# Residual update of a block moved into the next in-projection, and an out-projection of both halves at once

## The chip, the cores and the metric

The kernel runs on one core of a Trainium2 chip. The metric is the device time of one execution in microseconds (us), as a median over runs. Five engines work side by side: TensorE (PE; PEld is its weight load), VectorE (DVE), ScalarE (ACT), GpSimd (POOL) and SyncE (SP), on whose queue all the transfers stand. They meet through semaphores.

## The reference

Two layers (DEPTH) of a mixer with adaLN conditioning, over 2048 tokens of 1024 channels, in float32. Cut to what matters:

```python
for l in range(DEPTH):
    shift, scale, gate = split(silu(c) @ w_ada[l] + b_ada[l], 3)
    h = rms_norm(x, g_pre[l]) * (1 + scale) + shift
    u_a, b_a, c_a, gate_a, u_p, gate_p = split(h @ w_in[l])
    y_a = b_a * conv3(c_a * u_a, w_conv[l]) * silu(gate_a)
    y_p = pool(u_p, w_pool[l], pool_scale[l]) * silu(gate_p)
    y = concat([y_a, y_p]) @ w_out[l]
    x = x + gate * rms_norm(y, g_post[l])
```

Each of the six parts of the in-projection is 512 wide. The convolution and the pooling (windows of 2, 4, 8 and 16 tokens) look back in time.

## The kernel before

**Layout and stages.** x lies transposed: channels on the 128 partitions (KT = 8 channel tiles), tokens along the free axis. Work goes in four blocks: layer 0 and 1, each with two blocks of TB = 1024 tokens (two halves of HS = 512). A block has an in-projection, `in_phase`, and an out-projection. The in-projection has 24 groups of 128 output columns (six kinds, four of each); a group is one block of weights against the normalised h of both halves. The product is made in three passes (high x high, high x low, low x high), as every float32 operand is split into a part of the matmul's type and the rest: `mm_k` (L257) issues 8 channel tiles x 3 passes x 2 halves = 48 matmuls of 512 columns for a group. Each group is evicted and mixed on ACT and VectorE by the `use_` functions, ending in y, split in its turn.

**Weights.** `load_w` loads 512 KB (raw), ACT casts the high part (L98), and POOL subtracts for the low part (L108), in two halves of the contraction.

**Out-projection.** `out_half` goes over the eight groups of w_out for one half of the tokens, 24 matmuls a group, and is called twice for a block, so that w_out is loaded twice. Its result stays in SBUF in eight yo tiles. The epilogue, put off by `later` and released by `tick` during the groups that follow, makes 1 / rms of y (`rsqrt_mean`: a matmul with ones, Ln and Exp on ACT, one Newton step on VectorE), then for each channel tile y times it (L435), times the gate plus x (L436), the square (ACT L204) and its sum (VectorE L205) for the next layer's norm, and writes x1 to DRAM.

**Prenorm.** Between the two calls, the main loop queues the prenorm of the next block by `later`: x is loaded again, L234 on VectorE scales it, L235 on ACT adds the shift and rounds to h's high part, L240 on VectorE makes the low part.

**Order.** The scheduler sorts each engine's instructions; `pin` keeps a few in program order. The start (`start`, block 0) is in hand-written order on TensorE, VectorE and ACT: it works on half 0 as inputs arrive. Seven groups of weights are resident by its end; `in_phase` then runs half 1 for them. The last block (`out_last`) keeps w_out on chip and does its second half in two quarters of 256 columns. `background` is a list of steps (w_up times w_pool, adaLN rows, x statistics) handed out over the groups of an in-projection.

**Pools.** PSUM has eight banks: six single tiles for products (psm) and two for the rest (psa). `wsp` has four buffers of half a block of weights, `xpool` three buffers of two channel tiles, `t2` fifteen temporaries of 528 columns.

Of the kernel before, what the change touches and what calls it, by code (L numbers as in the profile page):

```python
# [9 lines left out]
I32 = mybir.dt.int32  # L10
# [3 lines left out]
P = 128  # L14
# [16 lines left out]
RSQRT_SEED = 1597463007.0  # L31
# [3 lines left out]
def trunk(ctx: ExitStack, tc: tile.TileContext, xt, c, wada, vec, rcp, win, wupt, wpool, wout, out):  # L35
# [5 lines left out]
    wsp = ctx.enter_context(tc.tile_pool(name="wsp", bufs=4))  # L41
    xpool = ctx.enter_context(tc.tile_pool(name="xpool", bufs=3))
    t2 = ctx.enter_context(tc.tile_pool(name="t2", bufs=15))
    dram = ctx.enter_context(tc.tile_pool(name="dram", bufs=1, space=bass.MemoryType.DRAM))
    psm = ctx.enter_context(tc.tile_pool(name="psm", bufs=6, space=bass.MemoryType.PSUM))
    psa = ctx.enter_context(tc.tile_pool(name="psa", bufs=2, space=bass.MemoryType.PSUM))

    def tmp(name, dtype=F32):
        return t2.tile([P, HALO + HS], dtype, tag="t", name=name)
# [23 lines left out]
    x1 = [dram.tile([P, KT, HS], F32, name=f"x1_{s}") for s in range(T // HS)]  # L73
# [36 lines left out]
    def load_w(src, dst=None, raw=None, defer=None, behind=None):  # L110
# [16 lines left out]
        return ws
# [29 lines left out]
    def rsqrt_short(ps, n, r, between=None):
        """1 / sqrt(ps + eps) by a short chain: exp(-ln / 2) and one Newton step."""
# [10 lines left out]
        newton(r, v, a, 1)  # L169
        return r  # L170

    def mean_begin(acc, e_hi=nc.vector, e_lo=nc.vector):
        ah = tmp("ah", F32R)
        al = tmp("al", F32R)
        split(acc, ah[:, :HS], al[:, :HS], e_hi, e_lo)
        return ah[:, :HS], al[:, :HS]

    def mean_mm(parts):
        ps = psa.tile([P, HS], F32, tag="aux", name="ps_stat")
        pin(nc.tensor.matmul(ps, lhsT=ones, rhs=parts[0], start=True, stop=False))  # L180
        pin(nc.tensor.matmul(ps, lhsT=ones, rhs=parts[1], start=False, stop=True))
        return ps

    def rsqrt_mean(parts, name, short):
        """1 / sqrt(mean + eps) on every partition, from the split sums of squares per partition."""
        ps = mean_mm(parts)
        if short:
            return rsqrt_short(ps, HS, tmp(name)[:, :HS])
        v = tmp("rs_v")[:, :HS]
        nc.vector.tensor_scalar(v, ps, EPS, None, op0=ALU.add)  # L190
        r = tmp(name)[:, :HS]
        a = tmp("rs_a")[:, :HS]
        nc.vector.tensor_scalar(a.bitcast(I32), v.bitcast(I32), 1, None, op0=ALU.logical_shift_right)
        nc.vector.tensor_scalar(r.bitcast(I32), a.bitcast(I32), -1.0, RSQRT_SEED, op0=ALU.mult, op1=ALU.add)
        newton(r, v, a, 3)
        return r

    def accumulate_sq(acc, src, first):
# [20 lines left out]
    def x_stats(s):
        acc = tmp("xacc")[:, :HS]  # L220
# [527 lines left out]
```

## Time and profile before

| | |
|---|---|
| median of 3 runs | 1516.43 us (1515.33 to 1517.26) |
| profiled execution, its span from first to last instruction | 1513.6 us |
| mean granted TensorE clock | 0.987 |
| TensorE busy | 1461.3 us, 97% of the span |
| VectorE busy | 871.0 us, 58% |
| ScalarE busy | 431.6 us, 29% |
| GpSimd busy | 473.7 us, 31% |
| chain that ended last | PE 79%, DVE 16% |
| DMA | 169.49 MB, 112 GB/s on average |

The profiled execution has no time of its own beside its span; the span leaves out what lies before the first and after the last instruction. Busy shares are averages over stages with different limits. The chain that ended last is followed back from the last instruction to what released it. The ends of matmuls are modelled, so that TensorE can look busy where it runs slowly; matmuls counted in a stretch tell more than its busy time. The granted clock is given as a share of 2.4 GHz.

### The profile page before, as it was taken

Reading aid. Unit: us, or ns where it says so; the run is one execution under the profiler, and the core shown is the slowest. Engines: PE = TensorE matmul, PEld = TensorE weight load, DVE = VectorE, ACT = ScalarE, POOL = GpSimd, SP = SyncE. Lnnn points to the kernel's source line nnn. Section 1 sums busy time; section 2 is a strip of 40 time slices with the busy share of each in tenths; the row PEclk is TensorE's granted clock in tenths of the full one; section 3 lists DMA queues with packets and bytes.
Section 4 is the critical chain, followed back from the end, with each engine's and each line's share of the span. In section 5 each row is a group of like instructions: output and inputs, shape, how many; then the busy total and the mean of one; then the engine's idle time right before and its main releaser. Section 6 shows DMA issues by size and latency. Waiting matters only on the chain.

```text
span 1513.6 us, 16929 instructions
## 1 busy us (share of the span) xinstructions
PE 1461.3 (97%) x6532; PEld 1197.0 (79%) x6532; DVE 871.0 (58%) x1253; ACT 431.6 (29%) x743; POOL 473.7 (31%) x324
## 2 busy tenths in 40 slices
PE   8899999999899999999979999999989999999996
PEld 4688888887678888888858888888867888888896
DVE  7962453869994556362799753352289434425155
ACT  4231211254632121114463121112444111111421
POOL 4510322244432222224534222223433222222501
PEclk9999999999999999999999999999999999999998
DMA  7421233443663332232465321111365411111223
GB/s 307 161 84 53 88 113 102 131 136 117 218 213 119 97 98 90 91 112 84 148 223 172 125 70 56 42 56 56 98 202 181 132 42 56 42 56 42 84 71 110
DMA packets 57684, 169.49 MB, mean 112 GB/s; under 512 B 5634, under 2 KB 9730, under 8 KB 57604
## 3 DMA queue, kind: packets, MB, share of 16 engines
q1 hardware_dynamic: 57604, 168.41, 33.8%
q8 instruction: 51, 0.84, 0.2%
q14 instruction: 29, 0.24, 0.0%
HBM read 147.42 MB, written 20.97 MB: 111 GB/s over the span
## 4 chain that ended last, share of the span: by engine, by line
PE 79%; DVE 16%; issue 2%; DMA 1%; ACT 1%; SPq 0%; DVEq 0%; ACTq 0%
PE ps_in L257 63%; PE ps_out L257 14%; DVE xin L234 3%; DVE h L240 2%; DVE xin L436 1%; DVE ada L130 1%; DVE yo L435 1%; DVE yacc L205 1%; DVE x L234 1%; PE ps_wu L286 1%; DVE rs_a L154 1%; DVE xacc L205 1%; DVE rs_a L153 1%; DVE rn L155 1%; DMA xin<-x 0%
## 5 line engine op out<-in xcount | busy, mean ns | idle before, releaser
L257 PE MATMUL ps_in<-h,ws 128*128 128x512 f32 x4368 | 1008.2, 392 | 22.9 <-ACT h L235 17.6
L257 PEld LDWEIGHTS ps_in<-h,ws 128*128 128x128 f32 x4368 | 822.4, 189 | 202.3 <-ACT h L235 22.6
L108 POOL TENSOR_TENSOR ws<-raw,ws 128x512 fp32r<-128x512 f32 x282 | 420.2, 1493 | 949.0 <-ACT ws L98 949.0
L98 ACT CAST ws<-raw 128x512 fp32r<-128x512 f32 x282 | 174.2, 621 | 572.6 <-PE ps_in L257 297.6
L257 PE MATMUL ps_out<-y,ws 128*128 128x512 f32 (+1 forms) x1296 | 291.5, 384 | 10.8 <-ACT ws L98 6.0
L257 PEld LDWEIGHTS ps_out<-y,ws 128*128 128x128 f32 x1296 | 237.7, 189 | 62.9 <-ACT ws L98 8.2
L205 DVE TENSOR_TENSOR yacc<-yacc,sq 128x512 f32<-128x512 f32 (+1 forms) x62 | 57.2, 923 | 111.9 <-ACT sq L204 111.6
L322 DVE COPY hu<-u 128x16 f32<-128x16 f32 x32 | 5.6, 176 | 178.7 <-ACT u L321 177.8
L368 DVE TENSOR_TENSOR cv<-cv,sga 128x512 f32<-128x512 f32 x32 | 21.9, 724 | 125.3 <-ACT sga L367 125.3
L343 DVE SCALAR_TENSOR_TENSOR pd<-pd,vecs,sgp 128x512 f32<-128x512 f32 x32 | 24.1, 795 | 81.0 <-ACT sgp L342 81.0
L257 PE MATMUL ps_out<-y,wh 128*128 128x256 f32 (+1 forms) x432 | 68.0, 319 | 0.0
L257 PEld LDWEIGHTS ps_out<-y,wh 128*128 128x128 f32 x432 | 61.9, 191 | 5.7
L257 PE MATMUL ps_in<-h,w 128*128 128x512 f32 x240 | 60.1, 401 | 1.0 <-DVE z L353 0.9
L234 DVE SCALAR_TENSOR_TENSOR xin<-xin,apre,rn 128x512 f32<-128x512 f32 x48 | 54.2, 1174 | 3.9 <-DMA xin<-x 3.9
L363 DVE TENSOR_TENSOR cv<-ps_in,cv 128x512 f32<-128x512 f32 x32 | 20.8, 685 | 61.6 <-PE ps_in L257 61.6
L257 PEld LDWEIGHTS ps_in<-h,w 128*128 128x128 f32 x240 | 46.7, 195 | 11.9 <-DVE z L353 1.4
L436 DVE SCALAR_TENSOR_TENSOR xin<-yo,gg,xin 128x512 f32<-128x512 f32 x56 | 52.3, 965 | 1.9 <-DMA xin<-x 1.2
L327 DVE TENSOR_TENSOR win<-win 128x525 f32<-128x525 f32 (+2 forms) x48 | 49.3, 1026 | 1.4
L422 ACT COPY yo<-ps_out 128x512 f32<-128x512 f32 x56 | 32.5, 580 | 58.1 <-PE ps_out L257 58.0
L235 ACT ACTIVATE h<-xin,mod 128x512 fp32r<-128x512 f32 x48 | 33.9, 723 | 42.2 <-DVE xin L234 42.2
L435 DVE TENSOR_TENSOR yo<-yo,ry 128x512 f32<-128x512 f32 x56 | 44.7, 833 | 0.2
L130 DVE SCALAR_TENSOR_TENSOR adaw<-adaw,cb 128x1024 f32<-128x1024 f32 x32 | 44.2, 1388 | 0.0
(112 smaller groups left out, 898.7 us busy)
## 6 DMA issues: line engine op xcount, KB each, us to landing
raw<-win SPq DMA_DIRECT2D x80, 512.0 KB, 3.5
raw<-wout SPq DMA_DIRECT2D x56, 512.0 KB, 3.5
adaw<-wada SPq DMA_DIRECT2D x32, 512.0 KB, 4.0
xin<-xt SPq DMA_DIRECT2D x32, 512.0 KB, 4.5
xin<-x SPq DMA_DIRECT2D x28, 512.0 KB, 4.3
ada<-wada SPq DMA_DIRECT2D x16, 512.0 KB, 8.9
raw<-wu SPq DMA_DIRECT2D x16, 512.0 KB, 3.2
x<-xin SPq DMA_DIRECT2D x16, 512.0 KB, 3.4
```

Of the source, the lines that this page charges most:

```text
L98: i = nc.scalar.copy(hi, src)
L108: e_lo.tensor_tensor(lo, src, hi.bitcast(F32), op=ALU.subtract)
L130: return nc.vector.scalar_tensor_tensor(w, w, 1.0, cb, op0=ALU.mult, op1=ALU.mult, accum_out=mod[:, l, j : j + 1])
L205: nc.vector.tensor_tensor(acc, acc, q, op=ALU.add)
L234: nc.vector.scalar_tensor_tensor(u, u, apre[:, l, k : k + 1], r, op0=ALU.mult, op1=ALU.mult)
L235: nc.scalar.activation(hs[k // 2][:, 0, k % 2, :], u, AF.Identity, bias=mod[:, l, k : k + 1])
L240: nc.vector.scalar_tensor_tensor(lo, u, mod[:, l, k : k + 1], hi, op0=ALU.add, op1=ALU.subtract)
L257: nc.tensor.matmul(ps[s], lhsT=ws[k // KH][:, wi, k % KH, :], rhs=rhs(k, ri, s), start=first and (wi, ri) == PASSES[0], stop=last and (wi, ...
L327: nc.vector.tensor_tensor(nxt[:, lo:], cur[:, lo:], cur[:, lo - w : HALO + HS - w], op=ALU.add)
L422: nc.scalar.copy(t, ps)
L435: nc.vector.tensor_tensor(yo[k], yo[k], r, op=ALU.mult)
L436: nc.vector.scalar_tensor_tensor(t[:, kk], yo[k], gg[:, l, k : k + 1], t[:, kk], op0=ALU.mult, op1=ALU.add)
```

## The change

1. `out_half` becomes `out_phase`: one pass over w_out for both halves (48 matmuls a group), with pair tiles in PSUM of two banks each, three for products and one for the rest.
2. In it, gated y (times gg) goes to DRAM (`ysp`) from ACT, group by group, and its squares are summed. The prenorm of the next block is done here too, in groups 1 to 4; the statistics of its x are ready by then: made in the background of the in-projection, by `x_stat_step` for block 1 and by `finish_steps` for layer 1.
3. `finish_steps`: eight steps in the background of the next in-projection load y and x of a channel tile, multiply by 1 / rms, add, write x1 (or the output), square and accumulate. Two buffers serve them in turn.
4. Work on VectorE and ACT is 1024 wide where it was 512. Temporaries: eight of 1040 columns.
5. The low parts of weights are made on VectorE, 1024 wide (in the start still on POOL). `wsp` has two buffers of a whole block.
6. The groups of the in-projection go in the order ua, up, ca, gp, ba, ga for each i, except in the first block. The split of y has its high part on ACT.
7. `rsqrt_mean`'s long form (an integer seed and three Newton steps) goes; Identity on ACT makes mean + eps.
8. `out_last`: its first half is updated 1024 wide behind group 0 of the first quarter; POOL has no part in the update any more.

The core of the diff:

```diff
-    wsp = ctx.enter_context(tc.tile_pool(name="wsp", bufs=4))
+    wsp = ctx.enter_context(tc.tile_pool(name="wsp", bufs=2))
-    t2 = ctx.enter_context(tc.tile_pool(name="t2", bufs=15))
+    t2 = ctx.enter_context(tc.tile_pool(name="t2", bufs=8))
-    psm = ctx.enter_context(tc.tile_pool(name="psm", bufs=6, space=bass.MemoryType.PSUM))
-    psa = ctx.enter_context(tc.tile_pool(name="psa", bufs=2, space=bass.MemoryType.PSUM))
+    psm = ctx.enter_context(tc.tile_pool(name="psm", bufs=3, space=bass.MemoryType.PSUM))
+    psa = ctx.enter_context(tc.tile_pool(name="psa", bufs=1, space=bass.MemoryType.PSUM))
...
+    IN_ORDER = [(kind, i) for i in range(NCG) for kind in ("ua", "up", "ca", "gp", "ba", "ga")]
...
+    def out_phase(l, b, y, nl, nb):
+        acc = tmp("yacc")[:, :TB]
+        log_exp()
+        h = []
+        rn = None
+        for j in range(KT):
+            ws = load_w(wout[l, j])
+            ps = pair_ps("ps_out")
+            for n, k in enumerate(range(KT) if j else OUT_ORDER):
+                mm_k(ws, [ps[:, 0], ps[:, 1]], y_rhs(y, 0, HS), k, n == 0, n == KT - 1)
+            if j == 0:
+                st = mean_mm(xparts[nl, nb])
+                rn = rsqrt_short(st, TB, tmp("rn")[:, :TB])
+            pf = flat(ps)
+            t = tmp("yg")[:, :TB]
+            nc.scalar.activation(t, pf, AF.Copy, scale=gg[:, l, j : j + 1])
+            accumulate_sq(acc, pf, j == 0)
+            nc.sync.dma_start(ysp[l, b][:, j], t)
+            for k in ((), (0, 1), (2, 3), (4, 5), (6, 7), (), (), ())[j]:
+                hk = hpool.tile([P, 2, TB], F32R, tag=f"h{k}", name=f"h{k}")
+                h.append(hk)
+                u = xpool.tile([P, TB], F32, tag="x", name="xin")
+                nc.sync.dma_start(u, x_src(nl, k, nb * TB, TB))
+                prenorm_hi(hk[:, 0], nl, k, u, rn)
+                prenorm_lo(hk[:, 0], hk[:, 1], nl, k, u)
+        parts = mean_begin(acc)
+        return parts, lambda k, ri, s: h[k][:, ri, s * HS : (s + 1) * HS]
...
+    def finish_steps(l, b):
+        st = {}
+        def step(k):
+            e = ypool.tile([P, 2, TB], F32, tag=("y3", "y7")[k % 2], name="fin")
+            nc.sync.dma_start(e[:, 0], ysp[l, b][:, k])
+            nc.sync.dma_start(e[:, 1], x_src(l, k, b * TB, TB))
+            nc.vector.tensor_tensor(e[:, 0], e[:, 0], ry[l, b], op=ALU.mult)
+            nc.vector.tensor_tensor(e[:, 1], e[:, 1], e[:, 0], op=ALU.add)
+            if l + 1 < DEPTH:
+                nc.sync.dma_start(x1[b][:, k], e[:, 1])
+                if k == 0:
+                    st["acc"] = tmp("xacc")[:, :TB]
+                accumulate_sq(st["acc"], e[:, 1], k == 0, e[:, 0])
+                if k == KT - 1:
+                    xparts[l + 1, b] = mean_begin(st["acc"])
+            else:
+                nc.sync.dma_start(out_dst(k, b * TB, TB), e[:, 1])
+        return [lambda k=k: step(k) for k in range(KT)]
...
+            def stat(pl=pl, pb=pb, parts=parts):
+                st = mean_mm(parts)
+                ry[pl, pb] = rsqrt_short(st, TB, tmp("ry")[:, :TB])
+            bg += [stat] + finish_steps(pl, pb)
```

**A boundary, VectorE.** The first out-projection, from the update of its first half to the prenorm, before (L108 and L107 are the split for the statistics, L205 sums squares):

```order
L435 TENSOR_TENSOR yo<-yo,ry 128x512 x2
L436 SCALAR_TENSOR_TENSOR xin<-yo,gg,xin 128x512
L205 TENSOR_TENSOR xacc<-xacc,sq 128x512
L436 SCALAR_TENSOR_TENSOR xin<-yo,gg,xin 128x512
L205 TENSOR_TENSOR xacc<-xacc,sq 128x512 x2
L107 CAST ah<-xacc 128x512
L108 TENSOR_TENSOR al<-xacc,ah 128x512
L234 SCALAR_TENSOR_TENSOR xin<-xin,apre,rn 128x512 x2
L240 SCALAR_TENSOR_TENSOR h_2529<-xin,mod,h_2529 128x512 x2
L234 SCALAR_TENSOR_TENSOR xin<-xin,apre,rn 128x512 x2
L205 TENSOR_TENSOR yacc<-yacc,sq 128x512
L240 SCALAR_TENSOR_TENSOR h_2533<-xin,mod,h_2533 128x512 x2
```

After, from out group 0 on (L145 to L147 are the Newton step, L218 and L222 the prenorm, L188 sums squares, L97 on ws makes a low part of weights):

```order
L145 SCALAR_TENSOR_TENSOR rs_a<-rs_v,rn 128x1024
L146 TENSOR_TENSOR rs_a<-rs_a,rn 128x1024
L147 SCALAR_TENSOR_TENSOR rn<-rs_a,rn 128x1024
L218 SCALAR_TENSOR_TENSOR xin<-xin,apre,rn 128x1024 x3
L222 SCALAR_TENSOR_TENSOR h_2075<-xin,mod,h_2075 128x1024
L222 SCALAR_TENSOR_TENSOR h_2081<-xin,mod,h_2081 128x1024
L222 SCALAR_TENSOR_TENSOR h_2147<-xin,mod,h_2147 128x1024
L188 TENSOR_TENSOR yacc<-yacc,sq 128x1024
L218 SCALAR_TENSOR_TENSOR xin<-xin,apre,rn 128x1024
L97 TENSOR_TENSOR ws<-raw,ws 128x1024
L222 SCALAR_TENSOR_TENSOR h_2153<-xin,mod,h_2153 128x1024
L218 SCALAR_TENSOR_TENSOR xin<-xin,apre,rn 128x1024 x2
```

The update has gone from here, and the prenorm's eight tiles stand between the low parts of the weights of out groups 2, 3 and 4.

**The start, VectorE.** From the Newton step for half 1's norm, before (L234 and L240 are the prenorm):

```order
L153 SCALAR_TENSOR_TENSOR rs_a<-rs_v,rn 128x512
L154 TENSOR_TENSOR rs_a<-rs_a,rn 128x512
L155 SCALAR_TENSOR_TENSOR rn<-rs_a,rn 128x512
L234 SCALAR_TENSOR_TENSOR x_381<-x_381,apre,rn 128x512 x2
L240 SCALAR_TENSOR_TENSOR h_555<-x_381,mod,h_555 128x512
L234 SCALAR_TENSOR_TENSOR x_381<-x_381,apre,rn 128x512
L240 SCALAR_TENSOR_TENSOR h_555<-x_381,mod,h_555 128x512
```

After (L317 to L326 are z and the convolution of the first group, L218 and L222 the prenorm):

```order
L145 SCALAR_TENSOR_TENSOR rs_a<-rs_v,rn 128x512
L317 COPY z<-hz_96 128x2
L319 TENSOR_TENSOR z<-ps_in,ua 128x512
L146 TENSOR_TENSOR rs_a<-rs_a,rn 128x512
L324 TENSOR_SCALAR cv<-z,vecs 128x512
L147 SCALAR_TENSOR_TENSOR rn<-rs_a,rn 128x512
L325 SCALAR_TENSOR_TENSOR cv<-z,vecs,cv 128x512
L218 SCALAR_TENSOR_TENSOR x_362<-x_362,apre,rn 128x512 x2
L326 SCALAR_TENSOR_TENSOR cv<-z,vecs,cv 128x512
L222 SCALAR_TENSOR_TENSOR h_533<-x_362,mod,h_533 128x512
```

z and the convolution have moved ahead of the prenorm and between the Newton operations.

**The end, VectorE.** The last block, from the first half's statistics on, before (L435 and L436 update the first half, L494 and L205 on 256 columns evict a quarter's group):

```order
L155 SCALAR_TENSOR_TENSOR ry<-rs_a,ry 128x512
L494 TENSOR_SCALAR yg<-ps_out,gg 128x256
L435 TENSOR_TENSOR yo<-yo,ry 128x512 x2
L436 SCALAR_TENSOR_TENSOR xin<-yo,gg,xin 128x512 x2
L435 TENSOR_TENSOR yo<-yo,ry 128x512 x2
L436 SCALAR_TENSOR_TENSOR xin<-yo,gg,xin 128x512 x2
L435 TENSOR_TENSOR yo<-yo,ry 128x512 x2
L436 SCALAR_TENSOR_TENSOR xin<-yo,gg,xin 128x512 x2
L435 TENSOR_TENSOR yo<-yo,ry 128x512 x2
L205 TENSOR_TENSOR yacc<-yacc,sq 128x256
L494 TENSOR_SCALAR yg<-ps_out,gg 128x256
```

After (L461 and L462 update the first half, L492 and L188 on 256 columns evict):

```order
L145 SCALAR_TENSOR_TENSOR rs_a<-rs_v,ry 128x512
L492 TENSOR_SCALAR yg<-ps_out,gg 128x256
L146 TENSOR_TENSOR rs_a<-rs_a,ry 128x512
L188 TENSOR_TENSOR yacc<-yacc,sq 128x256
L147 SCALAR_TENSOR_TENSOR ry<-rs_a,ry 128x512
L492 TENSOR_SCALAR yg<-ps_out,gg 128x256
L461 TENSOR_TENSOR yg<-yg,ry 128x1024 x2
L462 TENSOR_TENSOR xl<-xl,yg 128x1024 x2
L461 TENSOR_TENSOR yg<-yg,ry 128x1024 x2
L462 TENSOR_TENSOR xl<-xl,yg 128x1024
L188 TENSOR_TENSOR yacc<-yacc,sq 128x256
L492 TENSOR_SCALAR yg<-ps_out,gg 128x256
```

Operations are 1024 wide instead of 512, and seven of eight stand ahead of the third group's eviction where fourteen narrow ones stood.

## Rows read from the trace of the kernel before

**Rows 1.** The page: busy time by engine; the last chain by engine.

```profile
PE 1461.3 (97%) x6532; PEld 1197.0 (79%) x6532; DVE 871.0 (58%) x1253; ACT 431.6 (29%) x743; POOL 473.7 (31%) x324
...
PE 79%; DVE 16%; issue 2%; DMA 1%; ACT 1%; SPq 0%; DVEq 0%; ACTq 0%
```

**Rows 2.** The chain in order of time (start us, us, what).

```profile
86.91 8.23 PE ps_in L257 x35
...
392.10 2.43 DVE xin L234 x2
...
418.59 5.38 PE ps_in L257 x11
...
460.86 1.78 PE ps_wu L286 x16
...
500.04 184.31 PE ps_in L257 x813
...
1456.95 22.91 PE ps_out L257 x191
```

**Rows 3.** TensorE by line, 309:500, 675:860, 1040:1200 (busy, mean | idle).

```profile
L257 PE MATMUL ps_out<-y,ws 128*128 128x512 f32 x384 | 89.0, 391 | 2.5 <-POOL ws L108 2.2 <-ACT ws L98 0.3
L257 PE MATMUL ps_in<-h,ws 128*128 128x512 f32 x341 | 82.7, 400 | 4.8 <-ACT h L235 2.6 <-DVE h L240 1.1 <-POOL ws L108 0.7
L286 PE MATMUL ps_wu<-wp,wupt 128*128 128x128 f32 x64 | 8.3, 277 | 0.1
...
L257 PE MATMUL ps_out<-y,ws 128*128 128x512 f32 x384 | 88.8, 391 | 2.5 <-POOL ws L108 2.2 <-ACT ws L98 0.3
L257 PE MATMUL ps_in<-h,ws 128*128 128x512 f32 x369 | 87.0, 395 | 5.2 <-ACT h L235 2.5 <-DVE h L240 1.5 <-POOL ws L108 0.7
...
L257 PE MATMUL ps_out<-y,ws 128*128 128x512 f32 x384 | 90.2, 396 | 5.9 <-ACT ws L98 5.5 <-POOL ws L108 0.3
L257 PE MATMUL ps_in<-h,ws 128*128 128x512 f32 x262 | 61.9, 397 | 2.1 <-ACT h L235 1.6 <-DVE h L240 0.4
```

**Rows 4.** Stretches (PE, PEld, DVE, ACT, POOL busy; clock, DMA, GB/s).

```profile
62.00:66.00 4.00, 1.55 (x4) 1.28 (x5) 4.00 (x5) 1.23 (x2) 2.11 (x2) 0.66 0.00 0
66.00:70.00 4.00, 4.00 (x11) 3.17 (x10) 3.21 (x6) 0.72 (x1) 0.59 (x1) 0.50 0.00 0
410.00:420.00 10.00, 6.37 (x24) 4.20 (x23) 10.00 (x12) 5.65 (x10) 4.19 (x3) 0.91 0.70 213
1127.00:1137.00 10.00, 6.86 (x19) 5.01 (x20) 9.53 (x10) 6.04 (x11) 4.67 (x3) 0.66 0.64 222
```

**Rows 5.** Groups by line and form (busy us, mean ns | idle).

```profile
L108 POOL TENSOR_TENSOR ws<-raw,ws 128x512 fp32r<-128x512 f32 x282 | 420.2, 1493 | 949.0 <-ACT ws L98 949.0
...
L234 DVE SCALAR_TENSOR_TENSOR xin<-xin,apre,rn 128x512 f32<-128x512 f32 x48 | 54.2, 1174 | 3.9 <-DMA xin<-x 3.9
...
L180 PE MATMUL ps_stat<-ah,ones 128*128 128x512 f32 x14 | 6.3, 448 | 3.1 <-DVE ah L107 3.1
...
L205 DVE TENSOR_TENSOR yacc<-yacc,sq 128x256 f32<-128x256 f32 x13 | 5.5, 421 | 6.1 <-ACT sq L204 6.1
...
L108 DVE TENSOR_TENSOR al<-yacc,ah 128x512 fp32r<-128x512 f32 x7 | 4.8, 692 | 0.2
```

**Rows 6.** DMA issues (count, KB, us to landing).

```profile
xin<-x SPq DMA_DIRECT2D x28, 512.0 KB, 4.3
...
x<-xin SPq DMA_DIRECT2D x16, 512.0 KB, 3.4
```

**Rows 7.** Timeline of the start, ACT and DVE (start, us).

```profile
75.63 0.72 ACT L235 ACTIVATE h<-x,mod 128x512 fp32r<-128x512 f32 x1 [3.23 <-DVE x L234]
...
77.06 0.75 DVE L234 SCALAR_TENSOR_TENSOR x<-x,apre,rn 128x512 f32<-128x512 f32 x1
```

**Rows 8.** Timeline of the end, DVE.

```profile
1504.49 2.36 DVE L507 TENSOR_TENSOR yg<-yg,ry 128x512 f32<-128x512 f32 x2
...
1509.05 0.68 DVE L507 TENSOR_TENSOR yg<-yg,ry 128x512 f32<-128x512 f32 x1
```

More of the change, by code (lines that the diff above doesn't have):

```diff
@@ L168, in rsqrt_short, with mean_begin, mean_mm, accumulate_sq @@
             between()
-        newton(r, v, a, 1)
+        newton(r, v, a)
         return r
[L172 to L181, printed above, removed]
-        return ps
[L184 to L198, printed above, removed]
+    def mean_begin(acc, e_hi=nc.scalar, e_lo=nc.vector):
+        n = acc.shape[-1]
+        ah = tmp("ah", F32R)[:, :n]
+        al = tmp("al", F32R)[:, :n]
+        split(acc, ah, al, e_hi, e_lo)
+        return ah, al
+    def mean_mm(parts, ps=None):
+        n = parts[0].shape[-1]
+        if ps is None:
+            ps = flat(psa.tile([P, NH, HS], F32, tag="aux", name="ps_stat"))[:, :n]
+        for o in range(0, n, HS):
+            for i in range(2):
+                pin(
+                    nc.tensor.matmul(
+                        ps[:, o : o + HS], lhsT=ones, rhs=parts[i][:, o : o + HS], start=i == 0, stop=i == 1
+                    )
+                )
+        return ps
+    def accumulate_sq(acc, src, first, sq=None):
         if first:
@@ new lines, in rest @@
+            for k in range(KT):
+                o = slice(k * P, (k + 1) * P)
+                nc.tensor.matmul(ps[:, o], lhsT=raw[0][:, o], rhs=wp[l][:, g, :], start=True, stop=True)
+            keep = tmp("wk")[:, :D]
+            nc.scalar.copy(keep, ps)
+            nc.sync.dma_start(wu[l, g], keep.rearrange("p (a b) -> p a b", b=P))
+        return [load, rest]
+    START_ORDER = [("ua", 0), ("ua", 1)] + [(kind, i) for i in range(2) for kind in ("ca", "ba", "ga")]
+    START_ORDER += [(kind, i) for i in range(2) for kind in ("up", "gp")]
@@ L464, in load @@
             else:
[L465 to L474 removed]
+                t = hpool.tile([P, 2, KT, P], F32R, tag=f"h{j - 2}", name="wh")
@@ new lines, in load, with finish @@
+                wr[j] = load_w(wout[l, j], (t[:, :, :KH], t[:, :, KH:]), behind=last_act[0])
+        pending = []
+        def finish(yg, ps, nt, o, xs, r):
+            for q in range(4):
+                t = xs[q]
+                g = yg[q]
+                nc.vector.tensor_tensor(g, g, r.unsqueeze(1).broadcast_to([P, 2, nt]), op=ALU.mult)
+                nc.vector.tensor_tensor(t, t, g, op=ALU.add)
+                nc.sync.dma_start(out_dst(2 * q, o, nt, 2).rearrange("(k p) t -> p k t", p=P), t)
@@ L689, in trunk @@
-        if (l, b) == (1, 0):
-            bg += [lambda k=k: ada_late(1, 2 * KT + k) for k in range(KT)]
-            bg += [lambda: ada_fin(1, 2, 0, KT)]
-        y = in_phase(l, b, hb, bg, started if n == 0 else None)
+        if before is not None:
+            pl, pb, parts = before
+            def stat(pl=pl, pb=pb, parts=parts):
+                st = mean_mm(parts)
+                ry[pl, pb] = rsqrt_short(st, TB, tmp("ry")[:, :TB])
+            bg += [stat] + finish_steps(pl, pb)
+        more = []
@@ L695, in trunk @@
             break
-        out_half(l, b * NH, y, 0)
-        nl, nb = blocks[n + 1]
-        hb = [new_h(s) for s in range(NH)]
-        for q in range(KT // 2):
-            def pre(q=q, nl=nl, nb=nb, hb=hb):
-                for s in range(NH):
-                    prenorm(nl, nb * NH + s, hb[s], q)
-            later(2 + q, pre)
-        out_half(l, b * NH + 1, y, 1)
+        parts, hrhs = out_phase(l, b, y, *blocks[n + 1])
+        before = (l, b, parts)
 def kernel(**inputs):
```

487 lines of the change are left out of this document (221 added, 266 removed).

## The prediction

> **What bounds the kernel now.** I read the page's busy shares and chain first. TensorE is busy 97% of the span and carries 79% of the chain, VectorE 16% [rows 1]; so the question is in which stretches VectorE's 16% lies. The chain in order of time tells it: its long pieces are in-projections in which nothing but TensorE counts: 813 matmuls in 184.31 us [rows 2], 0.2267 us for a matmul of 512 columns, is one of them. A group of 48 thus takes 10.9 us. No gain is to be had there: the products are the same after the change.
>
> Next, TensorE by line over the three stretches that hold an out-projection and the start of the next in-projection [rows 3]. For each I take the length and subtract the matmuls at the steady rate (the 128-wide ps_wu ones at 0.111 us: 16 take 1.78 us in the chain [rows 2]; of the 14 ps_stat matmuls on a high part [rows 5] and as many on a low part, 12, 6 and 4 lie in the three):
> - 309 to 500: 191 - (384 + 341 + 12) x 0.2267 - 64 x 0.111 = 16.8 us lost.
> - 675 to 860: 185 - (384 + 369 + 6) x 0.2267 = 12.9 us lost.
> - 1040 to 1200: 160 - (384 + 262 + 4) x 0.2267 = 12.6 us lost.
>
> Together **42.3 us**. The idle time ahead of the ps_in matmuls (4.8, 5.2 and 2.1 us) ends with h. The rest of the loss is slow running: stretches of 10 us there hold 24 and 19 matmuls where 44 would fit, the granted clock averages 0.91 and 0.66, and VectorE is busy 10.00 and 9.53 of the 10 us [rows 4]. So VectorE bounds the boundaries: the residual update of the first half (L435, L436, L205), the rsqrts and the next block's prenorm (L234, L240) follow each other on it during the second half's out-projection; the prenorm starts at 392.10 in the chain, and TensorE has the chain again at 418.59 [rows 2].
>
> **The change, part by part.** *Boundaries.* The update leaves the boundary; the prenorm moves into out groups 1 to 4, one pair of channel tiles in each, before the out-projection ends. It can, as the statistics of the next block's x are made during the in-projection before. Does VectorE fit there? A two-input operation takes 692 ns at 512 columns and 421 ns at 256 where it stands alone [rows 5]: 271 ns for 256 columns, so about 1.23 us at 1024 (an estimate, no row has the 1024-wide form). An out group of 10.9 us has one low part of the weights, one yacc, and two pairs of L218 and L222: six operations, 7.5 us. In the new order (the fences on the boundary) the weights' low part of group m+2 comes behind group m's prenorm; adding up rows, it is ready 3 to 4 us before it is wanted. So I cost it at nothing; the cover is that margin. The y write adds a DMA of 512 KB for each group on SP's queue, x is read as before, and w_out is read once for a block instead of twice, so that DMA work stays about equal. **-42.3 us**; it could be less (the rival on VectorE below), not more.
>
> *In-projections.* They gain the update: 8 steps of three 1024-wide operations (y*ry, x+, accumulate), the low parts of 24 weight groups, an rsqrt of 1024. In the second block, the heaviest, I count 24 x 1.23 for low parts, 8 x 3 x 1.23 for steps, about 61 us for the mixer's own, 16 adaLN rows and the rsqrt: some 143 us of 24 x 10.9 = 262 us. POOL's pieces of 1493 ns [rows 5] go, and two of them with the wait for the cast made a weight ready later than one VectorE operation does. The stat matmuls run behind in-group 0, and the low part for in-group 2 waits behind the first Newton step on VectorE: Ln, Identity, Exp, one Newton operation and the low part, some 6 to 7 us, against 10.9 us of in-group 1. The steps load y and x into two buffers; a write takes 3.4 us and a load 4.3 us to land [rows 6], against about 20 us between steps. **0 us**.
>
> *Start.* Up to half 0's last matmul the order is unchanged. Then half 1's h waits for rn. Before, three Newton steps ran back to back, the first h began on ACT at 75.63, and the prenorm's operations followed on VectorE at 0.75 us each [rows 7]. In the new order (second pair of fences) the first group's z, which waits for TensorE and for ACT's copy of ua, and the convolution's operations stand between the Newton steps, and ACT makes Identity, two ua copies, a table load and sga first. Adding rows: rn at about 79.1, first h near 81.3, last h lo near 92. PSUM now comes in three pair tiles, so that only one of the three groups of half 1 has a place until VectorE has emptied the others, behind the prenorm; the 48 matmuls of the other two then follow: 92.2 + 10.9 = 103.1. Before, this point was reached when the chain's piece of ps_in from 86.91 ended, at 95.1 [rows 2]. That is +8; the pause may also bring the clock down, as 62 to 70 shows (0.66 where TensorE ran 1.55 of 4 us, then 0.50, the lower of its two levels, 1.2 GHz) [rows 4], for 0 to 3 us more. **+9 us**, bounds 0 (the z operations slip between waits) and +12.
>
> *Tail.* In the last quarters TensorE has three PSUM places instead of six. Counted from the end E of the last half: group 0 of the quarter ends at E + 2.9 (24 matmuls; 191 took 22.91 us [rows 2]), stat and ACT's chain to E + 5.7, Newton and two evictions to E + 9.2, then seven finish operations of 1.23 us stand before the third eviction (third pair of fences), which ends near E + 18.7. TensorE wants that place at E + 15: **+3.5 us**. The update of the first half, the fourth x tile that now waits for a buffer, and the update's two buffers, which stay taken into the last groups, make 0 to 2 us more. At the very end POOL's share goes to VectorE: eight operations of about 0.69 us instead of four of 1.18 beside POOL and two of 0.68 [rows 8]: -0.4 us, taking Identity's move to ACT against it. **+4 us**, bounds 0 and +6.
>
> **The sum:** -42.3 + 9 + 4 = -29.3 us. The profiled execution's span is 1513.6 us, the median of the runs 1516.43, 2.8 us outside the span; so a span near 1484, and **1487 us**.
>
> One rule bears on the 1.23 us. Rows first: the same L507 took 1.18 us a piece at 1504.49 with POOL's two operations beside it, and 0.68 us at 1509.05 alone [rows 8]. The Trainium skill (SBUF — State Buffer, Who interferes with whom) says that a VectorE instruction with two SBUF inputs contends with a GpSimd instruction that reads SBUF; the trace agrees, 1.18 against 0.68. After the change POOL reads nothing behind the start, so by that rule the short durations hold and the sum stays; by contended ones it would be rival 1's 1508.
>
> **The rivals.**
> 1. *VectorE is late inside the out-projection.* With contended lengths (L234 had 1174 ns on average, 1.6 times the 0.75 of its short row [rows 5, 7]) an out group's six operations would take 12 us, over 10.9; four groups in each of three boundaries lose 1.1 us and the low part behind them is late by as much again. For it: VectorE's rows are full at the boundaries now [rows 4]. Against: POOL is quiet. Some 7 us at each boundary come back, 21 in all: 1508.
> 2. *The start and the tail cost nothing:* 1516.4 - 42.3 = 1474. For it: the idle stretches I add are worked out from an order, and 1 to 2 us of slip each way would fill part of them.
> 3. *Slower: a low part queued behind an update step.* VectorE starts its rows in the order of the program. A step waits for y and x, and its buffer for the x1 write of two steps before: 3.4 + 4.3 = 7.7 us [rows 6]. If steps run in a burst, the next weight's low part stands behind that wait. With a margin of 3 us, TensorE loses 4.7 us for each of 24 steps, 113 us: 1600. It decides from 29.3 / 24 = 1.2 us a step. Against: steps lie about two groups apart, and loads have long landed by then. The Trainium skill (TensorE: Matmul & The Clock Gate, Architectural detail) calls the queues of ACT and DVE strict FIFO, the rule behind this rival; the trace of before shows no update step behind which a weight waits, as POOL made the weights.
> 4. *No change:* the scheduler puts the prenorm back at the boundary's end. The order shows that it doesn't; what could remain is a new wait of the same length.
>
> **How the numbers follow.** The forecast with its own bounds, 1478 to 1497: 0.60. Rival 2, 1470 to 1478: 0.14. Rival 1, 1497 to 1513: 0.15. Slower: 0.07. No change: 0.04. The range takes the forecast, most of rival 2 and half of rival 1: 1471 to 1505. About 0.2%, 3 us, is what a measurement of this kernel can tell from no change; faster by more 0.89, within it 0.04, slower 0.07.
>
> **What would show it right.** The page of after: TensorE's busy time falls toward 1430 with the same matmuls, POOL nearly empty. The three boundary stretches lose under 2 us each by the count of [rows 3]. At 82 to 104 us TensorE is thin, and its last half-1 matmuls end near 103 instead of 95. In the first quarter there is one idle gap of 3 to 4 us, ended by an eviction on VectorE. Wrong: idle time in out groups 1 to 4 ended by VectorE's ws (rival 1), or in the in-projections' first 17 groups ended by ws behind the update (rival 3).

## The result, and the profile after

| | before | after |
|---|---|---|
| median (4 runs each, side by side) | 1515.88 us (1514.53 to 1517.26) | 1490.95 us (1488.31 to 1491.81) |
| ratio after / before | | 0.9835, 95% interval 0.9822 to 0.9849 |
| span of the profiled execution | 1513.6 us | 1490.0 us |

The kernel is 24.9 us faster; 1487 had been forecast. The page of the changed kernel, busy time and last chain by engine (against [rows 1]):

```profile
PE 1451.2 (97%) x6532; PEld 1197.2 (80%) x6532; DVE 729.3 (49%) x820; ACT 412.7 (28%) x461; POOL 37.5 (3%) x30
...
PE 94%; DVE 5%; ACT 0%; issue 0%; DVEq 0%; ACTq 0%
```

TensorE's share of the chain has gone from 79% to 94%, VectorE's from 16% to 5%. The chain in order of time (start us, us, what) says where that is so:

```profile
98.88 12.34 PE ps_in L230 x53
111.22 1.78 PE ps_wu L256 x16
...
336.94 76.16 PE ps_out L230 x336
413.10 10.88 PE ps_in L230 x48
...
782.11 250.24 PE ps_in L230 x1104
...
1382.41 46.49 PE ps_out L230 x216
```

From 98.88 us on, the end of the start, pieces of TensorE follow each other without a break through all three boundaries: out-projection, in-group 0, the statistics, in-group 1, and so on. 1104 matmuls take 250.24 us, 0.2267 each, the old steady rate [rows 2]. TensorE by line from 325 to 500 (busy us, mean ns | idle), the place of the first three lines of [rows 3]:

```profile
L230 PE MATMUL ps_out<-y,ws 128*128 128x512 f32 x384 | 87.4, 389 | 0.0
L230 PE MATMUL ps_in<-h,ws 128*128 128x512 f32 x350 | 80.9, 390 | 0.0
L256 PE MATMUL ps_wu<-wp,wupt 128*128 128x128 f32 x64 | 7.8, 275 | 0.0
```

No idle time is left, and the count gives 384 + 350 + 8 matmuls (the 8 are ps_stat) x 0.2267 + 64 x 0.111 = 175.3 us for a stretch of 175: nothing is lost.

Three differences make up the span. Between the first ps_wu (95.14 before, 111.22 after) and the start of the last out-projection (1409.67 and 1382.41) lie 1314.5 us before and 1271.2 after: **-43.3 us** for the boundaries. Up to that ps_wu the start is **+16.1 us** late. From the last out-projection to the end it was 103.9 us and is 107.6: **+3.7 us**. Together -23.5, and the spans differ by 23.6. The start varies by itself: in the traces of runs 4 to 10 below, which leave it as it is, the first ps_wu begins between 109.1 and 111.3, so it is 14 to 16 us late.

The start first. Two stretches of its timeline after (start us, us, engine, line, what, idle time ahead and what ended it), one for each rsqrt:

```profile
10.35 4.43 PE L557 MATMUL ps_start<-sq,onesf 128*128 128x512 f32 x6
...
14.62 5.31 PE L537 MATMUL ps_start<-wt,onesf 128*128 128x512 f32 x12
...
19.97 0.69 ACT L153 ACTIVATE rs_a<-ps_start,epsc 128x512 f32<-128x512 f32 x1 [8.99 <-PE ps_start L537]
```

```profile
76.01 0.40 PE L176 MATMUL ps_start<-al,ones 128*128 128x512 f32 x1
...
82.36 0.39 PE L230 MATMUL ps_start<-h,w 128*128 128x512 f32 x1
82.79 0.69 ACT L153 ACTIVATE rs_a<-ps_start,epsc 128x512 f32<-128x512 f32 x1 [7.61 <-PE ps_start L230]
...
89.70 0.79 PE L230 MATMUL ps_in<-h,ws 128*128 128x512 f32 x1 [6.95 <-ACT h L219]
```

Ln of the first rsqrt reads the statistics that are ready at 14.78 us, and starts only when twelve warm-up pieces behind them have ended; before it started at 14.11. Ln of the second is released by the last matmul of group 6 at 82.36, 6 us behind the statistics. In both cases the other writer has the other bank of one tile, `aux`, which the change made out of two tiles. Behind the second wait TensorE runs dry (stretches of 4 us; columns as in [rows 4]):

```profile
82.00:86.00 4.00, 0.75 (x4) 0.29 (x2) 1.40 (x4) 3.21 (x6) 0.00 (x0) 0.91 0.00 0
86.00:90.00 4.00, 0.30 (x1) 0.29 (x1) 4.00 (x7) 2.50 (x4) 0.00 (x0) 0.50 0.00 0
90.00:94.00 4.00, 3.56 (x8) 2.09 (x8) 4.00 (x7) 1.75 (x3) 0.00 (x0) 0.50 0.00 0
```

It stands nearly still for 7 us, and for the 8 us from 86 on the granted clock is 0.50, the lower of its two levels (1.2 GHz).

The tail, stretches of the last block after:

```profile
1440.00:1444.00 4.00, 1.90 (x15) 1.70 (x14) 4.00 (x8) 0.39 (x1) 0.00 (x0) 0.97 0.79 278
1444.00:1448.00 4.00, 4.00 (x24) 4.00 (x23) 1.99 (x4) 0.00 (x0) 0.00 (x0) 0.60 1.00 322
```

TensorE is busy 1.90 of 4 us in the first (its gap of 2.10 us is ended by yg L492, an eviction on VectorE), and the granted clock dips to 0.60 in the second. The dip doesn't always follow: the traces of runs 5, 7, 8 and 10 have the same gap of 2.1 us, and the 96 matmuls behind it take 11.78 us there instead of 13.26 (the chain of the changed kernel and of run 5):

```profile
1443.37 13.26 PE ps_out L230 x96
```

```profile
1445.13 11.78 PE ps_out L230 x96
```

### The profile page after: what moved, and what is told of

Read it like the earlier page. It is cut to its first block, busy times and chain, and to the rows that moved or that the text cites. A ratio compares the mean times of both kernels' runs of the same rounds, so it can differ in the third digit from the quotient of the medians.

```text
span 1490.0 us, 15524 instructions
## 1 busy us (share of the span) xinstructions
PE 1451.2 (97%) x6532; PEld 1197.2 (80%) x6532; DVE 729.3 (49%) x820; ACT 412.7 (28%) x461; POOL 37.5 (3%) x30
## 4 chain that ended last, share of the span: by engine, by line
PE 94%; DVE 5%; ACT 0%; issue 0%; DVEq 0%; ACTq 0%
PE ps_in L230 68%; PE ps_out L230 23%; DVE ada L124 1%; DVE x L218 1%; PE ps_wu L256 1%; PE ps_start L537 1%; DVE h L222 1%; DVE yg L461 0%; DVE apre L570 0%; PE ps_stat L176 0%; DVE xl L462 0%; PE ps_start L557 0%; PE ps_c L614 0%; DVE rs_a L146 0%; ACT rs_v L154 0%
## 5 line engine op out<-in xcount | busy, mean ns | idle before, releaser
L87 ACT CAST ws<-raw 128x1024 fp32r<-128x1024 f32 (+1 forms) x119 | 123.0, 1035 | 232.8 <-PE ps_in L230 182.7
L97 DVE TENSOR_TENSOR ws<-raw,ws 128x1024 fp32r<-128x1024 f32 x115 | 140.2, 1219 | 87.2 <-ACT ws L87 87.1
L188 DVE TENSOR_TENSOR yacc<-yacc,sq 128x1024 f32<-128x1024 f32 (+2 forms) x41 | 36.0, 878 | 140.9 <-ACT sq L187 140.9
L336 DVE TENSOR_TENSOR cv<-cv,sga 128x1024 f32<-128x1024 f32 (+1 forms) x17 | 19.7, 1161 | 113.8 <-ACT sga L335 113.8
L305 DVE SCALAR_TENSOR_TENSOR pd<-pd,vecs,sgp 128x1024 f32<-128x1024 f32 x16 | 20.5, 1284 | 76.3 <-ACT sgp L304 76.3
L335 ACT ACTIVATE sga<-ps_in 128x1024 f32<-128x1024 f32 (+1 forms) x17 | 16.6, 977 | 140.9 <-PE ps_in L230 140.8
L406 ACT ACTIVATE yg<-ps_out,gg 128x1024 f32<-128x1024 f32 x24 | 26.7, 1112 | 97.3 <-PE ps_out L230 97.3
L330 DVE TENSOR_TENSOR cv<-ps_in,cv 128x1024 f32<-128x1024 f32 (+1 forms) x17 | 19.2, 1128 | 56.8 <-PE ps_in L230 56.8
L187 ACT ACTIVATE sq<-ps_out 128x1024 f32<-128x1024 f32 (+2 forms) x41 | 30.5, 745 | 53.6 <-PE ps_out L230 53.6
L319 DVE TENSOR_TENSOR z<-ps_in,ua 128x1024 f32<-128x1024 f32 (+1 forms) x18 | 19.9, 1106 | 48.5 <-PE ps_in L230 48.5
```

What stands on the lines that cost most here:

```text
L87: i = nc.scalar.copy(hi, src)
L97: e_lo.tensor_tensor(lo, src, hi.bitcast(F32), op=ALU.subtract)
L187: nc.scalar.activation(q, src, AF.Square)
L188: nc.vector.tensor_tensor(acc, acc, q, op=ALU.add)
L305: nc.vector.scalar_tensor_tensor(m, m, vecs[:, l, V_PS + g : V_PS + g + 1], sg, op0=ALU.mult, op1=ALU.mult)
L319: nc.vector.tensor_tensor(z[:, 2 + o : 2 + o + n], ps, usb[i][:, o : o + n], op=ALU.mult)
```

## The experiments

Diffs are cut to the edit. Each result is the median, to be set beside 1490.95 us for the changed kernel.

**1. Warm-up in a tile of its own**, a pair of psm (`wps[0]`) until the groups take it.

```diff
-        nc.tensor.matmul(aux[:, 1, :c], lhsT=onesf, rhs=wt[:, :c], ...)
+        nc.tensor.matmul(wps[0][:, 1, :c], lhsT=onesf, rhs=wt[:, :c], ...)
```

> Only the warm-up matmuls of the start write into a PSUM tile of their own (a pair that the groups take later); the statistics keep the tile that group 6 shares. Theory, the shared tile: in the changed kernel Ln of the first rsqrt starts at 19.97 us, behind the twelve warm-up pieces that end at 19.9, where before it started at 14.11; with the tile apart it starts near 14.8 and all of the start comes 5 to 6 us earlier: 1485 us (1491 less 5.9). The second Ln (82.79) still waits for group 6, so the rest of the start's loss stays. Rival, the start is paced by its loads: Ln moves, but the last matmuls of half 1 stay near 111 us, 1491 us.

Measured: 1485.83 us, -5.1. ACT's timeline in that run:

```profile
14.38 0.69 ACT L153 ACTIVATE rs_a<-ps_start,epsc 128x512 f32<-128x512 f32 x1 [3.27 <-PE ps_start L558]
```

Ln starts 5.6 us earlier, behind the statistics, and the whole start comes with it (the first ps_wu at 106.2 instead of 111.2). The shared tile was the cause; the loads are not the pace.

**2. Statistics in a tile of their own too.** The pair `aux` becomes two tiles of one bank; statistics of 1024 columns and ps_wu take one after the other.

```diff
-    psa = ctx.enter_context(tc.tile_pool(name="psa", bufs=1, ...))
+    psa = ctx.enter_context(tc.tile_pool(name="psa", bufs=2, ...))
-        aux = psa.tile([P, NH, HS], F32, tag="aux", name="ps_start")
+        aux = [aux_ps("ps_start"), aux_ps("ps_in7")]
```

> Warm-up apart as in the other run, and the auxiliary PSUM pair is two single tiles, so that the statistics of half 1 and group 6 of the weights don't share one. Theory, the shared tile: the second Ln starts right behind the statistics' matmuls instead of behind group 6's last matmul, 6.4 us earlier, the scheduler puts the prenorm of half 1 ahead of z again, and the half-1 matmuls end near 95 to 98 us instead of 111: 1475 to 1478 us. Rival, the PSUM pairs: half 1's second and third group have no place before VectorE has emptied one, whatever Ln does, and this costs the 8 us that were forecast: the end of half 1 near 103 us, 1482 to 1485 us.

Measured: 1478.66 us, another -7.2. ACT's timeline:

```profile
70.21 0.69 ACT L159 ACTIVATE rs_a<-ps_start,epsc 128x512 f32<-128x512 f32 x1 [1.46 <-PE ps_start L182]
...
75.07 0.72 ACT L223 ACTIVATE h<-x,mod 128x512 fp32r<-128x512 f32 x1 [3.07 <-DVE x L222]
```

Ln starts at 70.21, released by the statistics, and h at 75.07 (before 75.63, [rows 7]). The order of the program changed with it: Newton's step and the prenorm stand ahead of z again, as before the change. So z had moved forward, it seems, because Ln was to come late: the order went back with the tile, but run 2 also splits Ln and ps_wu, and no run parts these.

**3. Two half-1 groups in one PSUM pair**, on top of 2.

```diff
-                ps1 = {n: pair_ps("ps_in")[:, 1] for n in part}
+                p01 = pair_ps("ps_in")
+                ps1 = {0: p01[:, 0], 1: p01[:, 1], 2: pair_ps("ps_in")[:, 1]}
```

> As the run with the statistics in a tile of their own (1478.66), and half 1's first two groups share one PSUM pair instead of taking half of a pair each. Theory, places in PSUM: in that run the half-1 matmuls of groups 0 to 2 end at 98.8 us where the kernel before had 95.0, because only one of three groups has a place during the prenorm; with two of them TensorE does 48 matmuls between the prenorm's tiles instead of 24 and ends near 94: 1474 us. Rival: the two groups now wait for each other's evictions through the shared tile, and it stays at 1478 to 1480.

Measured: 1474.67 us, another -4.0. The stretches 78 to 86 of run 2, and then of this run:

```profile
78.00:82.00 4.00, 3.28 (x13) 1.77 (x11) 4.00 (x7) 2.17 (x4) 0.00 (x0) 1.00 0.01 4
82.00:86.00 4.00, 2.93 (x10) 1.48 (x10) 4.00 (x8) 2.79 (x4) 0.00 (x0) 1.00 0.00 0
```

```profile
78.00:82.00 4.00, 4.00 (x19) 3.28 (x18) 4.00 (x7) 2.20 (x4) 0.00 (x0) 1.00 0.02 4
82.00:86.00 4.00, 4.00 (x20) 3.30 (x19) 4.00 (x9) 2.79 (x4) 0.00 (x0) 1.00 0.00 0
```

39 matmuls run there instead of 23, between the same prenorm operations: the number of places was worth those 4 us. With 1 to 3 the start has lost its 16 us.

**4. The tail's update spread**, one pair of channel tiles behind each group of the next quarter instead of all behind group 0.

```diff
-                if j == 0 and pending:
-                    pending.pop()()
+                if pending:
+                    pending.pop(0)()
```

> In the last block the update of the part before is handed out one pair of channel tiles for each group of the next quarter, instead of all behind group 0. Theory, VectorE's order: the idle gap of TensorE of 2.10 us that a quarter's eviction ends (1441.3 to 1443.4) goes, and with it the dip of the clock behind it (0.60 in 1444 to 1448, some 1.2 us): 1487.6 us. Rival, the end is set elsewhere (the last rsqrt, the output's transfer): the gap goes but the time stays, 1491 us.

Measured: 1486.76 us, -4.2. The same place of the tail in that run:

```profile
1438.00:1442.00 4.00, 4.00 (x36) 4.00 (x35) 4.00 (x6) 0.38 (x1) 0.00 (x0) 1.00 0.85 277
1442.00:1446.00 4.00, 4.00 (x36) 4.00 (x35) 3.17 (x7) 0.77 (x2) 0.00 (x0) 1.00 0.88 279
```

36 matmuls in each 4 us at clock 1.00: gap and dip are gone, and the last out-projection to the end takes 103.5 us instead of 107.6.

**5. Low parts of the weights on GpSimd.**

```diff
-        e_lo = e_lo or nc.vector
+        e_lo = e_lo or nc.gpsimd
```

> The low parts of all weights back on GpSimd, 1024 wide, nothing else. Theory, VectorE has room: it is 49% busy, a low part takes some 3 us on GpSimd and is wanted 10.9 us after its cast may start, so the time is the same within 4 us: 1491 to 1495. Rival, contention: GpSimd's reading lengthens VectorE's two-input operations to 1.6 times, six of them in an out-projection's group need 12 us instead of 7.5, over the 10.9 of a group, and the three boundaries lose 5 to 7 us each: 1506 to 1512 us, with TensorE idle in out groups 1 to 4. In either case the trace shows by how much the same VectorE forms lengthen.

Measured: 1490.90 us, no difference. Groups by line and form, of the changed kernel and then of this run:

```profile
L222 DVE SCALAR_TENSOR_TENSOR h<-xin,mod,h 128x1024 fp32r<-128x1024 f32 x24 | 30.1, 1281 | 4.0 <-ACT h L219 3.7
L218 DVE SCALAR_TENSOR_TENSOR xin<-xin,apre,rn 128x1024 f32<-128x1024 f32 x24 | 30.1, 1281 | 2.3 <-DMA xin<-xt 1.6 <-DMA xin<-x 0.6
...
L97 DVE TENSOR_TENSOR y<-pd,y 128x1024 fp32r<-128x1024 f32 x16 | 19.6, 1223 | 0.0
```

```profile
L97 POOL TENSOR_TENSOR ws<-raw,ws 128x1024 fp32r<-128x1024 f32 x115 | 295.0, 2565 | 1020.3 <-ACT ws L87 1020.3
...
L218 DVE SCALAR_TENSOR_TENSOR xin<-xin,apre,rn 128x1024 f32<-128x1024 f32 x24 | 39.0, 1657 | 3.4 <-DMA xin<-xt 2.1 <-DMA xin<-x 1.1
L97 DVE TENSOR_TENSOR y<-pd,y 128x1024 fp32r<-128x1024 f32 x16 | 33.5, 2094 | 12.7 <-ACT y L87 12.7
...
L222 DVE SCALAR_TENSOR_TENSOR h<-xin,mod,h 128x1024 fp32r<-128x1024 f32 x24 | 30.0, 1280 | 3.8 <-ACT h L219 3.7
```

The contention is real: y's low part grew from 1223 to 2094 ns, and of the prenorm L218 from 1281 to 1657, while L222 kept its 1280. It costs nothing that the median shows: only 0.7 us of TensorE's time waits for a low part of y, and 0.3 for one of the weights. Moving the low parts did nothing by itself. The rival's 12 us for an out group were not reached: one of the six operations is gone from VectorE, and of the rest only L218 is longer.

**6. The prenorm late**, with its rsqrt behind out group 6.

```diff
-            if j == 0:
+            if j == 6:
                 st = mean_mm(xparts[nl, nb])
-            for k in ((), (0, 1), (2, 3), (4, 5), (6, 7), (), (), ())[j]:
+            for k in ((), (), (), (), (), (), range(KT), ())[j]:
```

> The changed kernel with the rsqrt and the prenorm of the next block at out group 6 instead of groups 0 to 4; the residual update stays in the next in-projection. Theory, the place of the prenorm is what the boundary was about: rn comes some 2 to 3 us before the out-projection ends, then VectorE has eight pairs of 1024-wide operations (20 us) with low parts and sums between, TensorE gets h at 2.5 to 3 us a channel tile, and each of three boundaries loses 10 to 15 us plus a dip of the clock: 1521 to 1540 us, most of the 42 us back. Rival, moving the update alone made the room: the prenorm catches up within in-group 0 and the time stays within 5 us of 1491.

Measured: 1512.99 us, +22.0 or 7.3 a boundary, less than the theory's 10 to 15 and far from the rival's nothing. TensorE's timeline of that boundary and its waits:

```profile
414.31 9.45 PE L230 MATMUL ps_in<-h,ws 128*128 128x512 f32 x38 [1.55 <-DVE h L222]
426.35 9.27 PE L230 MATMUL ps_in<-h,ws 128*128 128x512 f32 x33 [2.59 <-DVE h L222]
```

```profile
PE ps_in L230 <- DVE h L222: 13.0, 11, 2.6
...
PE ps_in L230 <- DVE ws L97: 0.5, 2, 0.3
```

Between two waits it runs 38 and 33 matmuls. Three tiles of h, the number that L222 had made by 416.65, give one group 18; so more than one group at a time takes up each tile of h, which hides a part. The waits on h and on weights make up some 15 of the 22 us; the rest is slower running (from 424 to 432 the granted clock averages 0.77 and 0.80).

**7. Both: prenorm late, and low parts on GpSimd.**

> The run with the late prenorm (1512.99), and the low parts of all weights on GpSimd as well. Alone, GpSimd's low parts cost nothing (1490.90 against 1490.95), though single VectorE forms grew from 1.22 to 2.1 us. Theory, lengthened VectorE operations cost where VectorE stands on the path: with the prenorm late TensorE waits for h from VectorE for 2 to 4 us at a time, prenorm pairs beside a GpSimd subtraction take 1.66 instead of 1.28 us, and each of three boundaries loses 1 to 3 us more: 1516 to 1522 us. Rival, the loads of x through three buffers set the pace there (VectorE waits for them by 1.2 to 1.8 us at a time): the same within 2 us, 1511 to 1515.

Measured: 1519.27 us, +6.3 on run 6 and above the kernel before (1515.01 beside it). The time is the theory's, its mechanism isn't: L218 took 1280 ns in this run and 1282 in run 6. TensorE's waits name another:

```profile
PE ps_in L230 <- DVE h L222: 10.7, 12, 1.6
PE ps_in L230 <- POOL ws L97: 7.0, 7, 1.4
```

GpSimd's own 2.56 us a weight make the weights late (7.0 us in seven waits, 0.5 in run 6), while the waits for h shrink from 13.0 to 10.7.

**8. The update in bursts.** Its steps come first, and up to six steps of background a group.

```diff
-        y = in_phase(l, b, hrhs, [f for _, _, f in todo], ...)
+        y = in_phase(l, b, hrhs, bg + more, ...)
-                for f in background[: -(-len(background) // max(1, len(order) - 7 - n))]:
+                for f in background[: -(-len(background) // max(1, len(order) - (18 if before is not None else 7) - n))]:
```

> The changed kernel with the update's steps no longer spread over 17 groups of an in-projection but handed out first and in bursts (six, three and two steps of background a group in the three blocks, so that all eight steps lie in the first two to five groups). Theory, room and early loads: a round of two steps takes about a write (3.4), a load (4.9) and four operations (4.9), some 13 us against 10.9 of a group, so a weight's low part is late by a few us in four rounds of the first block or two: 1491 to 1501 us. Rival 3 of the prediction, the low parts queue behind each step's wait: 4.7 us for each of up to 24 steps, 1540 to 1600 us, with TensorE idle ended by VectorE's ws in the first five groups of the in-projections.

Measured: 1503.18 us, +12.2, just over the theory's range. The loss lies in the second block, the one with six steps a group: one wait of 12.23 us, and some 3 us of slow running behind it (granted clock 0.50 from 476 to 484), against a start and a tail that were 3.4 us shorter in this execution. The other two in-projections run at 250.28 and 250.26 us for 1104 matmuls. Timeline of the wait:

```profile
476.57 1.06 ACT L187 ACTIVATE fin<-fin 128x1024 f32<-128x1024 f32 x1 [5.22 <-issue]
...
479.88 1.01 ACT L258 COPY wk<-ps_wu 128x1024 f32<-128x1024 f32 x1
...
480.93 3.78 PE L256 MATMUL ps_wu<-wp,wupt 128*128 128x128 f32 x16 [12.23 <-ACT wk L258]
```

No weight's low part was late. TensorE's ps_wu needed the one auxiliary pair, whose eviction (wk) stood on ACT behind the square of an update step and a cast, and that square behind VectorE and the loads. Rival 3's kind of queue exists, on another engine and only in the burst.

**9. The out-projection in two halves again**, the rest as changed: 16 groups of 24 matmuls, prenorm behind groups 2 to 9.

```diff
-        for j in range(KT):
+        for sb, j in [(sb, j) for sb in range(2) for j in range(KT)]:
-                mm_k(ws, [ps[:, 0], ps[:, 1]], y_rhs(y, 0, HS), k, ...)
+                mm_k(ws, [ps[:, sb]], y_rhs(y, sb * HS, HS), k, ...)
```

> The changed kernel with the out-projection one half of the tokens at a time again (w_out loaded and split twice, 24 matmuls or 5.44 us a group, gated y written in halves); the prenorm goes on one channel tile a group behind out groups 2 to 9, the update stays in the next in-projection. Theory, a weight's low part is now due every 5.44 us and waits on VectorE behind the Newton step of rn: rn's chain ends some 8.5 us behind out group 1, the low part of group 3 about 12 us behind it and is wanted after 5.4, so each of three boundaries loses some 7 us once, and the prenorm's pace (4.5 of 5.44 us a group) costs no more: 1508 to 1515 us. Rival, what counts is that update and prenorm left the boundary, and w_out twice is hidden: 1491 to 1495 us.

Measured: 1492.38 us, ratio to before 0.9851 (0.9836 to 0.9865): no different from the changed kernel within the interval. The low part that stands behind the Newton step was group 4's, not group 3's as I had counted, and it came 0.24 us late instead of 7.

**10. Two halves, and low parts on GpSimd.**

> The same with the low parts of weights on GpSimd, where they don't queue behind the Newton step. Theory as for the other run: the loss at group 3 goes, a low part takes 2.6 us and its cast 1.05 of 5.44, what remains is up to 3 us a boundary: 1491 to 1500 us, faster than the other by 8 us or more. Rival, lengthened VectorE operations: one group's work of 4.5 us grows past 5.44 and this run is the slower of the two: over 1515 us.

Measured: 1510.00 us, +17.6 on run 9. Timeline, VectorE, ACT, GpSimd and TensorE:

```profile
343.82 5.81 DVE L218 SCALAR_TENSOR_TENSOR xin<-xin,apre,rn 128x1024 f32<-128x1024 f32 x3
...
347.27 2.35 ACT L219 ACTIVATE h<-xin,mod 128x1024 fp32r<-128x1024 f32 x2 [3.81 <-DVE xin L218]
...
351.62 1.04 ACT L87 CAST ws<-raw 128x1024 fp32r<-128x1024 f32 x1
...
352.73 6.61 POOL L97 TENSOR_TENSOR ws<-raw,ws 128x1024 fp32r<-128x1024 f32 x2 [6.58 <-ACT ws L87]
...
356.08 6.31 PE L230 MATMUL ps_out<-y,ws 128*128 128x512 f32 x14 [2.64 <-POOL ws L97]
```

At a weight each 5.44 us, two subtractions on GpSimd took 6.61 us beside VectorE's prenorm, and TensorE waited 2.64 us for them, once at each boundary (7.9 us in three; another 3.0 for low parts of y). The count from 325 to 500 lacks some 30 matmuls, or 7 us, against run 9 (376 + 324 and 377 + 354), as the granted clock falls to 0.50 behind the wait (356 to 360). It is the slower of the two, as the rival said, if not past its 1515. By these rows the weight is late from VectorE on: GpSimd stood idle for 6.58 us until ACT's cast, the cast came behind the prenorm's h on ACT, and h waited for L218, 1685 ns on average in this run and 1278 in run 9. GpSimd's own lengthened subtractions come on top.

**11. Start and tail mended** (1 to 4 together).

> All three mends together: warm-up and statistics in tiles of their own, two half-1 groups in one pair, the tail's update spread. Theory, the losses of start and tail are separate and add up: 1478.7 less 4.2 for the tail less 4 for the pair, 1470 to 1471 us. Rival, the tail's gain was one of position only and vanishes: 1474 to 1475 us.

Measured: 1471.31 us, ratio to before 0.9704 (0.9690 to 0.9719): 19.6 us faster than the changed kernel. The chain's last lines that answer to those above:

```profile
1028.53 76.18 PE ps_out L234 x336
...
1366.78 46.49 PE ps_out L234 x216
```

1104 matmuls and out-projections are as long as before; the last out-projection starts 15.6 us earlier and the end is 103.6 us behind it. The gains of start and tail add up.

## Why the prediction was right, and where it was off

- **Boundaries, -42.3 us:** measured -43.3, 1 us past the forecast's "not more". The cover held where VectorE was fullest, 10.62 of 11 us, and so did the margin of 3 to 4 us (a stretch, and the two low parts that stand between the prenorm's tiles):

```profile
358.00:369.00 11.00, 11.00 (x51) 9.09 (x50) 10.62 (x9) 6.55 (x7) 0.00 (x0) 1.00 0.78 256
```

```profile
354.57 1.22 DVE L97 TENSOR_TENSOR ws<-raw,ws 128x1024 fp32r<-128x1024 f32 x1
...
365.02 1.22 DVE L97 TENSOR_TENSOR ws<-raw,ws 128x1024 fp32r<-128x1024 f32 x1
```

 TensorE has 51 matmuls in the stretch. The low parts end at 355.8 and 366.2; their groups begin at 358.7 and 369.6 (48 matmuls or 10.88 us each, from 336.94). One reading of before was off: not all of the loss was VectorE's or slow running. 10.9 us of it were idle time ahead of ps_out, ended by weights from POOL and ACT [rows 3]. Which edit brought the gain: an early prenorm is worth 22 us in the new kernel (run 6). The other edits stand in for each other: low parts on VectorE are worth 0 beside an out-projection of both halves (run 5) and 17.6 beside two halves (run 10), two halves cost nothing clear with low parts on VectorE (run 9). What the update had cost at its old place, and what the 1024-wide operations bring, was not tried by itself; how the other 20 us are shared out stays open.
- **In-projections, 0:** right, 250.24 us for 1104 matmuls. The 1.23 us were measured as 1.22 for two tensors and 1.28 for the form with a scalar.
- **Start, +9 us:** measured +16.1; this is the term that was mis-sized. The step that failed is "Up to half 0's last matmul the order is unchanged": it was, and I took the times to be unchanged as well. What had changed are the waits, as statistics shared a tile with the warm-up and with group 6. That cost 5.1 and 7.2 us (runs 1 and 2), and the interleaved z went with it. The PSUM places cost 4.0 us (run 3): of the forecast's 9 us only these came by the way it named. The other 12 came by one that it did not have, and took the start past its bound of +12.
- **Tail, +4 us:** measured +3.7, by the step that was named: the third eviction behind seven operations. Of the 3.5 us of gap 2.1 came, and the clock's dip made up the rest, 1.5 us. That the sum fits is in part luck, as the dip is missing in four of the other traces.
- **The sum:** -29.3 forecast, -23.6 in the spans. The start's 7 us account for it, less 1 for the boundaries. TensorE's busy time came to 1451.2 instead of toward 1430: the idle times of [rows 3] add up to 23 of the 42.3 us, so that it could fall by 19 at most, and the later start adds 4.5 (85.8 us busy up to 111, before 81.3 up to 95).
- **Rivals:** rival 1 did not come: with POOL quiet L218 and L222 took 1281 ns each, and its contended lengths were not tried in full (run 5 lengthens one of the two). Rival 2's 1474 is what the mends bring (1471.3). Rival 3 needs a burst, and then it is ACT's queue (run 8). The Trainium skill (SBUF — State Buffer, Who interferes with whom) says that a VectorE instruction with two SBUF inputs contends with a GpSimd instruction that reads SBUF; run 5's lengthened forms agree, and no loss of time came of it there.

## What to carry to other kernels

An unchanged order of instructions is no proof of unchanged times: compare what each one waits for, above all where buffers were joined into one tile, since a reader of one half can then wait for the writer of the other (runs 1 and 2; in run 3 two groups shared a pair and lost nothing). Work that bounds a boundary should be moved to where its engine has room before the boundary, here the prenorm; a part that is worth nothing when undone alone can be worth 18 us beside another. And places for results (three pairs instead of six) show first where evictions queue behind long work.

## What the runs showed that I had not expected

- On GpSimd one subtraction of 1024 columns takes 2565 ns (run 5) where two of 512 took 1493 each [rows 5].
- A gap of 2.1 us on TensorE in the tail was followed by a granted clock of 0.60 over the next 4 us in one trace, while in run 5 the clock stayed at 1.00 behind the same gap; and the still stretch from 82 by 0.50 for 8 us, though matmuls had begun again at 89.7.
- With h late, TensorE ran 38 matmuls between two tiles' waits (run 6): the scheduler had put several groups side by side, which hid a part of what I had worked out.
